# Sums of the down weights tied to the weight loads, one sum in place, and a new order of the pools in a hybrid encoder block

## Chip, cores and metric

The kernel runs on one core of a Trainium2 chip. The metric is the device time of one execution in microseconds. Engines: TensorE (PE, with its weight loads PEld), VectorE (DVE), ScalarE (ACT), GpSimd (POOL) and SyncE (SP), which only issues DMAs.

## What is computed

One layer over 2048 positions of width 1024, in float32:

```
h   = rms_norm(x) * norm_mix_g
z   = h @ w_in                       # two head groups share one projection
A   = u * (W_s LN(v) + b)            # gated blocks of 128 positions
B   = softmax(q k^T / 8 + c[t] - c[s]) v, s <= t,  c = cumsum(log sigmoid(f))
x   = x + concat(A, B) @ w_out
a   = conv3(rms_norm(x) * norm_ffn_g @ w_up) + b_conv     # 1024 -> 2 x 2816, causal, per channel
x   = x + (silu(g) * v) @ w_down     # a = g, v ; 2816 -> 1024
out = rms_norm(x) * norm_final_g
```

## The kernel before, in words

**Numbers as pairs.** Every float32 operand of a product is split in a rounded part and a remainder (`hi`, `lo`), and each product is made of three matmuls: hi.hi, hi.lo, lo.hi. The split is an ACT copy and a DVE subtraction (`both`, line 913) or, for weights of the first stages, a POOL cast `whi` and a DVE subtraction `wlo` (`load_unit`, line 118). `load_unit` takes a raw buffer (2 of them), loads it on SP and remembers that DMA as `raw_ins`; there are 4 buffers each for `whi` and `wlo`.

**Order of the work.** A schedule is made when the program is built: a list scheduler simulates the engines, starts each instruction as soon as its operands and a buffer of its tag are there, prefers the earlier one in the program (or one under `high_priority`), and fixes the order on each engine. On the chip each engine, SP's DMA issues included, keeps that order and waits where it must. `issue_after(ins)` puts the instructions traced inside behind `ins` in the order of the engine that `ins` runs on; it adds no semaphore.

**Stages.** First the input projection of two halves of 1024 positions (`a_half`). Attention runs as a stream of small steps (`b_stream`) put between the matmuls of the other stages. Then for half 0 the output projection (`c_half`, line 782): for two blocks of 512 positions it loads mixed values `thi`, `tlo` (`load_mix`), loads the output weights by `load_unit`, multiplies, adds the input rows, stores the result and makes normalised rows `ar` with a POOL instruction. Then the up projection of half 0 (`d_half`, line 853): 22 blocks `f` of 128 channels, each with a gate and a value unit of weights (`units(f)`, two `load_unit`) and two calls of `d_up` (one for each block of positions), with convolution and gate on DVE and ACT and a store of the gated values on POOL's queue.

**Sums of down weights.** The down projection uses Strassen's scheme in Winograd's form, seven products in place of eight, so it needs four sums of quarters of the down weights for each of 11 pairs of blocks. `d_sums(i)` (line 880) makes them on POOL: it loads two 512 KB tiles `tw` (2 buffers, so one pair at a time; lines 885, 886), subtracts four times (line 893) and stores each sum to DRAM on POOL's queue (line 894). In the program it stands between the two `d_up` calls of every second block (for the first and last pair of blocks, between the two blocks of positions).

**Half 1.** `c_late` (line 924) is the output projection of half 1; it reads mixed values 2 from the first pair of `thi`/`tlo` buffers and mixed values 3 from the second, and its weights through the same raw buffers. `late_half` (line 970) then makes an up projection in the seven-product form: `up_raw` (line 1052) loads raw weights `rawl` (3 buffers), `up_gate` splits the gate weights for products P1 and P2 (`xg`), `up_sums` (line 1064) makes four sums `sf` and splits them for the other five products (`xs`), and `up_mms` (line 1084) multiplies. Results are kept in `pc` tiles (3 buffers). The positions' own sums (`T1` to `T4`, `Y22`) are made once, at the beginning, on ACT and DVE.

The pools of half 1 are laid out in the order in which they are opened, in memory that the earlier stages held: before, the raw weights come first (kept open until the end of the program), then `xpool` (`xg`, then `xs`, then `sf`), `y2pool`, and the `pc` tiles last. A new tile waits for those tiles that lay in the same place. From the start of that memory, the earlier stages had 8 KB per partition of raw buffers, then 32 KB of the first `thi`/`tlo`, then 32 KB of the second, then the split weights.

**Down projection.** `down` (line 1147) runs for both halves the products P1, P2, P7, P6, P5, P4, P3, each over 11 units. `prep` (line 1172) loads a unit's weights or sums (`wr`), splits them (`wh`, `wl`), loads quarters of the gated values (`x11`, `x12`, `x21`, `x22`, 11 buffers each), adds them where the product asks for it, and splits them (`xh`, `xl`). `ready(u + 2)` keeps preparation two units ahead of the matmuls (line 1214).

Of the kernel before, what the change touches and what calls it, by code (L numbers as in the profile page):

```python
# [48 lines left out]
}  # L49
# [6 lines left out]
class Block:  # L56
# [823 lines left out]
    def d_sums(self, i):  # L880

        nc, dp = self.nc, self.dp
        w_down = self.a["w_down"][0].rearrange("(f p) n -> p f n", p=P)
        w1, w2 = self.til(dp, [P, D], F32, "tw"), self.til(dp, [P, D], F32, "tw")
        self.dma(w1, w_down[:, i, :])
        self.dma(w2, w_down[:, i + NF // 2, :])
        t1 = self.til(dp, [P, TB], F32, "tn")
        y11, y12 = w1[:, 0:TB], w1[:, TB:D]
        y21, y22 = w2[:, 0:TB], w2[:, TB:D]
        tt = nc.gpsimd.tensor_tensor  # L890

        for k, out, a, b in ((0, t1, y12, y11), (2, y12, y22, y12), (1, y22, y22, t1), (3, y21, y21, y22)):
            tt(out, a, b, op=ALU.subtract)
            nc.gpsimd.dma_start(self.tw_d[k][i], out)
# [75 lines left out]
    def late_half(self, accp, close_c):  # L970
        nc, tc = self.nc, self.tc
        self.c_late(accp)
        close_c()
        kw = dict(bufs=1, reuse_waits="tile")
        es = ExitStack()
        self.rawp = self.ctx.enter_context(tc.tile_pool(name="rawlate", **kw))
        xp = self.xp = es.enter_context(tc.tile_pool(name="xpool", **kw))
        yp = es.enter_context(tc.tile_pool(name="y2pool", **kw))
        self.up = es.enter_context(tc.tile_pool(name="upool", **kw))
        self.upp = es.enter_context(tc.tile_pool(name="ups", space=PSUM, **kw))  # L980
        self.w_up = self.a["w_up"][0].rearrange("(c p) n -> p c n", p=P)
        self.X, self.ps, self.p1, self.raw, self.cv = {}, {}, {}, {}, {}
        (y11, y21), (y12, y22) = self.yf
        y = lambda n: [yp.tile([P, 4, TB], F32R, name=f"{n}{i}") for i in "hl"]
        T2, T3, T1, T4, Y22 = y("t2"), y("t3"), y("t1"), y("t4"), y("y22")
        self.Y = dict(P1=self.Y11, P2=self.Y21, P3=Y22, P4=T4, P5=T1, P6=T2, P7=T3)
        for c in range(2):
            self.up_raw(0, c)
        self.up_raw(1, 0)
        self.up_gate(0)  # L990
        self.up_gate(1)
        self.prod(0, "P1", "A")
        self.prod(0, "P2", "C")
        self.up_sums(0)
        self.up_raw(2, 0)
        self.up_raw(1, 1)
        self.up_gate(2)

        def first(c):
            v = lambda t: t[:, :, c]  # L1000
            tt = nc.vector.tensor_tensor
            tt(v(y11), v(y12), v(y11), op=ALU.subtract)
            tt(v(y12), v(y22), v(y12), op=ALU.subtract)
            self.both([v(t) for t in Y22], v(y22))
            tt(v(y22), v(y22), v(y11), op=ALU.subtract)
            self.both([v(t) for t in T2], v(y22))

        first(slice(0, 384))
        for k in range(2):
            self.turned(1, 3, self.row, k, self.tqp, "tq")  # L1010
        first(slice(384, 512))
        self.prod(1, "P1", "A")
        self.prod(1, "P2", "C")
        self.both(T3, y12)
        self.both(T1, y11)

        nc.vector.tensor_tensor(y21, y21, y22, op=ALU.subtract)
        self.both(T4, y21)
        self.prod(2, "P1", "A")
        self.prod(2, "P2", "C")  # L1020
        for f in range(NF):
            self.up_mms(f)
            if 0 < f < NF - 1:
                self.up_conv(f - 1)
        es.close()
        self.tqs.close()
        self.down()
# [36 lines left out]
    def up_sums(self, f):  # L1064
        nc = self.nc
        g, v = self.raw.pop((f, 0)), self.raw.pop((f, 1))
        a, b = slice(0, 512), slice(512, 1024)
        S = {n: [self.til(self.xp, [P, TB], F32R, "xs" + n + i) for i in "hl"] for n in ("P6", "P7", "P5", "P4", "P3")}
        F = {n: self.til(self.xp, [P, TB], F32, "sf") for n in ("P5", "P6", "P3", "P7")}
        s = lambda n: F[n]  # L1070
        tt = nc.vector.tensor_tensor
        tt(s("P5"), v[:, a], v[:, b], op=ALU.add)
        tt(s("P6"), s("P5"), g[:, a], op=ALU.subtract)
        tt(s("P3"), g[:, b], s("P6"), op=ALU.subtract)
        self.both(S["P6"], s("P6"))
        tt(s("P7"), g[:, a], v[:, a], op=ALU.subtract)
        self.both(S["P7"], s("P7"))
        self.both(S["P5"], s("P5"))
        self.both(S["P4"], v[:, b])
        self.both(S["P3"], s("P3"))  # L1080
        for n in S:
            self.X[f, n] = S[n]
# [64 lines left out]
    def down(self):  # L1147
# [24 lines left out]
        def prep(u):  # L1172
            half, n, j = units[u]
            w = self.til(dp, [P, TB], F32, "wr")
            src = dict(P1=w_down[:, j, 0:TB], P2=w_down[:, j + NJ, 0:TB], P3=w_down[:, j + NJ, TB:D],
                       P5=self.tw_d[0][j], P6=self.tw_d[1][j], P7=self.tw_d[2][j], P4=self.tw_d[3][j])[n]
            self.w_ins = self.dma(w, src).ins
            wp = [self.til(dp, [P, TB], F32R, "wh"), self.til(dp, [P, TB], F32R, "wl")]
            self.both(wp, w)
            x = lambda name: block(half, j, name)  # L1180
            if n == "P1":
                v = x("x11")
            elif n == "P2":
                v = x("x12")
            elif n == "P7":
                v = self.til(dp, [P, TB], F32, "xs")
                tt(v, x("x11"), x("x21"), op=ALU.subtract)
            elif n == "P6":

                tt(x("x21"), x("x21"), x("x22"), op=ALU.add)  # L1190
                v = x("x11")
                tt(v, x("x21"), v, op=ALU.subtract)
            elif n == "P5":
                v = x("x21")
            elif n == "P4":
                v = x("x22")
            else:
                v = self.til(dp, [P, TB], F32, "xs")
                tt(v, x("x12"), x("x11"), op=ALU.subtract)
            xp = [self.til(dp, [P, TB], F32R, "xh"), self.til(dp, [P, TB], F32R, "xl")]  # L1200
            self.both(xp, v)
            parts[u] = wp, xp
# [55 lines left out]
        for half in range(2):  # L1258
            for n in self.PRODUCTS:
                which, blk, col, whole = PLAN[n]  # L1260
                fresh = n in ("P1", "P2", "P7")
                if fresh:
                    banks[which] = [self.til(pp, [P, TB], F32, "D") for _ in range(4)]
                bank = banks[which]
                tail = {"P2": 2, "P6": 2, "P3": 4 if half else 2}.get(n, 0)
                cs = slice(col * TB, (col + 1) * TB)
                for j in range(NJ - tail):
                    ready(u + 2)
                    for t in range(4):
                        mms(bank, u, t, fresh, j == NJ - 1)  # L1270
                    u += 1
                    if (n, j) == ("P1", 4):
                        for t in range(4):
                            row(half, t)
                    if (n, j) == ("P2", 7):
                        for t in range(4):
                            row(half, 4 + t)
                for t in range(4):
                    if tail:
                        ready(u + tail + max(0, t - 1))  # L1280
                    for m in range(tail):
                        mms(bank, u + m, t, fresh, m == tail - 1)
                    x = row(half, 4 * blk + t)
                    tt(x[:, cs], bank[t], x[:, cs], op=ALU.add)
                    if whole:
                        square(half, 4 * blk + t, col)
                        if n in ("P4", "P3"):
                            end_row(half, 4 * blk + t)
                u += tail
# [55 lines left out]
```

## Time and profile before

| | |
|---|---|
| runs | 2522.92, 2529.30, 2529.84 us; median 2529.3 |
| profiled execution | 2528.71 us, of which the span from first to last instruction is 2527.0 |
| mean granted TensorE clock | 0.992 of 2.4 GHz |
| busy, share of the span | PE 97%, PEld 79%, DVE 69%, ACT 54%, POOL 14% |
| DMA | 396 MB, mean 157 GB/s |

PE's busy share is an average over stages; what matters is in which stages it has pauses and what ended them. The granted clock of a stretch is 1.00 when TensorE ran at 2.4 GHz all through it, and 0.5 at 1.2 GHz. Each wait is put down to what released it last.

### The profile page before, as it was taken

To read this page: it belongs to the slowest core of one execution; us is meant where nothing else is said; L and a number is where in the kernel's file an instruction comes from. 1 tells how busy PE (TensorE), PEld (TensorE's weight loads), DVE (VectorE), ACT (ScalarE), POOL (GpSimd) and SP (SyncE) were. 2 spreads that over 40 slices of the span, in tenths; PEclk is the share of its full clock that TensorE was granted. 3 is DMA by queue.
4 is the path that set the end of the run, shared out by engine and by line. 5 is a ranking of instruction groups with operands and counts; after the bars stand their busy time and mean duration, and the time that the engine had idled before them with its cause. 6 is when DMAs were issued, how large, how long until landed. Compare 5 with 4: busy or idle time off the path is not lost.

```text
span 2527.0 us, 33250 instructions
## 1 busy us (share of the span) xinstructions
PE 2448.3 (97%) x11082; PEld 1998.6 (79%) x11082; DVE 1750.6 (69%) x3119; ACT 1360.0 (54%) x2628; POOL 360.1 (14%) x402
## 2 busy tenths in 40 slices
PE   8999989999999999999999999989999999999997
PEld 6887877878777788888888888868888887888886
DVE  5237676565556877777777775488888877858766
ACT  4327777554344555667676672254554455444443
POOL 3204122000356511100010011100000000001000
PEclk9999999999999999999999999999999999999999
DMA  6863534666978744444444445412222227538633
GB/s 184 261 163 100 165 110 123 182 174 190 303 263 274 237 130 130 142 140 136 136 140 147 138 125 193 157 53 81 92 84 79 88 93 275 167 97 308 189 110 113
DMA packets 348567, 396.10 MB, mean 157 GB/s; under 512 B 53964, under 2 KB 223124, under 8 KB 348380
## 3 DMA queue, kind: packets, MB, share of 16 engines
q1 hardware_dynamic: 338188, 359.37, 46.9%
q0 software_dynamic: 10208, 34.61, 3.5%
q8 instruction: 88, 1.44, 0.2%
q14 instruction: 83, 0.68, 0.1%
HBM read 300.30 MB, written 93.72 MB: 156 GB/s over the span
## 4 chain that ended last, share of the span: by engine, by line
PE 79%; DMA 7%; DVE 5%; ACT 4%; POOL 2%; issue 2%; SPq 0%; POOLq 0%; DVEq 0%; ACTq 0%
PE D L1214 17%; PE mm L174 11%; PE mm L176 11%; PE mm L178 11%; PE A L1043 3%; PE A L1042 3%; PE A L1044 3%; PE o L722 2%; PE o L721 2%; DMA tw<-in_w_down_dram 2%; PE B L1043 2%; PE B L1044 2%; PE B L1042 2%; PE s L673 2%; PE s L672 1%
## 5 line engine op out<-in xcount | busy, mean ns | idle before, releaser
L174 PE MATMUL mm<-thi,whi 128*128 128x512 f32 x960 | 378.5, 394 | 1.3 <-DVE vn L384 1.3
L178 PE MATMUL mm<-thi,wlo 128*128 128x512 f32 x960 | 377.6, 393 | 0.9 <-DVE wlo L128 0.9
L176 PE MATMUL mm<-tlo,whi 128*128 128x512 f32 x960 | 377.3, 393 | 0.0
L174 PE MATMUL mm<-whi,thi 128*128 128x512 f32 x640 | 254.2, 400 | 7.1 <-DMA thi<-mixh 3.1
L176 PE MATMUL mm<-wlo,thi 128*128 128x512 f32 x640 | 254.7, 398 | 2.7 <-DVE wlo L128 2.6
L178 PE MATMUL mm<-whi,tlo 128*128 128x512 f32 x640 | 253.5, 396 | 0.0
L1214 PE MATMUL D<-wh,xh 128*128 128x512 f32 x616 | 236.2, 389 | 3.0 <-ACT xh L915 3.0
L1214 PE MATMUL D<-wl,xh 128*128 128x512 f32 x616 | 236.7, 389 | 0.0
L1214 PE MATMUL D<-wh,xl 128*128 128x512 f32 x616 | 235.9, 389 | 0.0
L681 ACT ACTIVATE s<-s,part 128x512 f32<-128x512 f32 (+3 forms) x257 | 150.5, 586 | 141.6 <-DVE part L676 81.9
L174 PEld LDWEIGHTS mm<-thi,whi 128*128 128x128 f32 x960 | 181.0, 189 | 40.2 <-DVE vn L384 2.0
L178 PEld LDWEIGHTS mm<-thi,wlo 128*128 128x128 f32 x960 | 180.9, 188 | 39.0 <-DVE wlo L128 1.4
L176 PEld LDWEIGHTS mm<-tlo,whi 128*128 128x128 f32 x960 | 181.1, 189 | 37.8
L116 POOL TENSOR_SCALAR whi<-raw 128x1024 fp32r<-128x1024 f32 x108 | 121.5, 1126 | 621.6 <-PE mm L178 200.5
L128 DVE TENSOR_TENSOR wlo<-raw,whi 128x1024 fp32r<-128x1024 f32 x108 | 138.6, 1284 | 59.3 <-POOL whi L116 59.1
L745 DVE TENSOR_TENSOR pl<-e,ph 128x512 fp32r<-128x512 f32 (+2 forms) x212 | 139.5, 666 | 55.6 <-ACT ph L744 31.2
L739 ACT ACTIVATE e<-s 128x512 f32<-128x512 f32 (+2 forms) x227 | 115.4, 528 | 107.4 <-DVE s L737 56.6
L174 PEld LDWEIGHTS mm<-whi,thi 128*128 128x128 f32 x640 | 121.3, 190 | 33.5 <-POOL whi L116 4.0
L176 PEld LDWEIGHTS mm<-wlo,thi 128*128 128x128 f32 x640 | 121.6, 190 | 28.8 <-DVE wlo L128 5.8
L178 PEld LDWEIGHTS mm<-whi,tlo 128*128 128x128 f32 x640 | 121.2, 190 | 23.9
L1214 PEld LDWEIGHTS D<-wh,xh 128*128 128x128 f32 x616 | 115.5, 188 | 27.5 <-ACT xh L915 3.4
L1214 PEld LDWEIGHTS D<-wl,xh 128*128 128x128 f32 x616 | 115.5, 188 | 24.2 <-DVE wl L916 0.4
(1092 smaller groups left out, 5566.7 us busy)
## 6 DMA issues: line engine op xcount, KB each, us to landing
m<-kx SPq DMA_DIRECT2D x133, 256.0 KB
raw<-in_w_up_dram SPq DMA_DIRECT2D x44, 512.0 KB
rawl<-in_w_up_dram SPq DMA_DIRECT2D x44, 512.0 KB
x<-act SPq DMA_DIRECT2D x88, 256.0 KB
wr<-tw SPq DMA_DIRECT2D x88, 256.0 KB
m<-kx SPq DMA_DIRECT2D x160, 136.0 KB
raw<-in_w_in_dram SPq DMA_DIRECT2D x40, 512.0 KB
v<-vd SPq DMA_DIRECT2D x66, 256.0 KB
```

Source lines behind the costliest of these rows:

```text
L116: self.cast_ins = self.nc.gpsimd.tensor_scalar(out, in_, 1.0, 0.0, ALU.mult, ALU.add).ins
L128: nc.vector.tensor_tensor(lo, raw, f32(hi), op=ALU.subtract)
L174: mm(ps, lhsT=ah[k], rhs=bh[k], start=k == 0, stop=False)
L176: mm(ps, lhsT=ah[k], rhs=bl[k], start=False, stop=False)
L178: mm(ps, lhsT=al[k], rhs=bh[k], start=False, stop=k == n - 1)
L681: nc.scalar.activation(ps[:, :n], ps[:, :n], AF.Exp, scale=-1.0, bias=dst, accum_out=ls[:, tt, sb:sb + 1])
L739: nc.scalar.activation(e[:, c], ps[:, c], AF.Exp, scale=-1.0)
L745: nc.vector.tensor_tensor(pl[:, c], e[:, c], f32(ph[:, c]), op=ALU.subtract)
L1042: mm(ps, lhsT=xh[:, ks], rhs=yh[:, k, :], start=fresh and k == 0, stop=False, **kw)
L1043: mm(ps, lhsT=xh[:, ks], rhs=yl[:, k, :], start=False, stop=False, **kw)
L1044: mm(ps, lhsT=xl[:, ks], rhs=yh[:, k, :], start=False, stop=k == 3, **kw)
L1214: nc.tensor.matmul(bank[t], lhsT=x[i][:, ts], rhs=w[k], start=fresh and j == 0 and i + k == 0, stop=last and i == 1, **kw)
```

## The change

The two `tw` loads of `d_sums` are issued behind the last raw weight load traced before them. In `late_half`, the pool of the `pc` tiles is opened first, the pool of the raw weights second, and the latter now closes with the others; the four `sf` tiles are allocated before the `xs` tiles; `pc` has 4 buffers. In `prep`, the difference `x12 - x11` is written into `x12` during product P5, and P3 uses it from there. In product P3 of half 1, preparation runs four units ahead.

```
-    ... "pc": 3, "A": 3, "B": 1, "C": 3,
+    ... "pc": 4, "A": 3, "B": 1, "C": 3,
@@ d_sums
-        self.dma(w1, w_down[:, i, :])
-        self.dma(w2, w_down[:, i + NF // 2, :])
+
+        with self.tc.issue_after(self.raw_ins):
+            self.dma(w1, w_down[:, i, :])
+            self.dma(w2, w_down[:, i + NF // 2, :])
@@ late_half
-        self.rawp = self.ctx.enter_context(tc.tile_pool(name="rawlate", **kw))
+
+        self.up = es.enter_context(tc.tile_pool(name="upool", **kw))
+        self.rawp = es.enter_context(tc.tile_pool(name="rawlate", **kw))
         xp = self.xp = es.enter_context(tc.tile_pool(name="xpool", **kw))
         yp = es.enter_context(tc.tile_pool(name="y2pool", **kw))
-        self.up = es.enter_context(tc.tile_pool(name="upool", **kw))
@@ up_sums
+        F = {n: self.til(self.xp, [P, TB], F32, "sf") for n in ("P5", "P6", "P3", "P7")}
         S = {n: [self.til(self.xp, [P, TB], F32R, "xs" + n + i) for i in "hl"] for n in ("P6", "P7", "P5", "P4", "P3")}
-        F = {n: self.til(self.xp, [P, TB], F32, "sf") for n in ("P5", "P6", "P3", "P7")}
@@ prep
             elif n == "P5":
                 v = x("x21")
+
+                tt(x("x12"), x("x12"), x("x11"), op=ALU.subtract)
             elif n == "P4":
                 v = x("x22")
             else:
-                v = self.til(dp, [P, TB], F32, "xs")
-                tt(v, x("x12"), x("x11"), op=ALU.subtract)
+                v = x("x12")
@@ down
-                    ready(u + 2)
+                    ready(u + (4 if (half, n) == (1, "P3") else 2))
```

## Rows read from the trace of the kernel before

**Rows 1.** The page's chain that ended last, by line.

```profile
PE D L1214 17%; PE mm L174 11%; PE mm L176 11%; PE mm L178 11%; PE A L1043 3%; PE A L1042 3%; PE A L1044 3%; PE o L722 2%; PE o L721 2%; DMA tw<-in_w_down_dram 2%; PE B L1043 2%; PE B L1044 2%; PE B L1042 2%; PE s L673 2%; PE s L672 1%
```

**Rows 2.** Stages: length, busy PE PEld DVE ACT POOL (instructions), clock, DMA share, GB/s.

```profile
668.00:796.00 128.00, 118.96 (x525) 94.73 (x524) 74.20 (x132) 54.18 (x125) 73.64 (x72) 0.96 0.83 269
796.00:889.00 93.00, 85.46 (x370) 67.89 (x369) 76.40 (x112) 49.21 (x100) 50.01 (x52) 0.94 0.76 242
889.00:1510.00 621.00, 621.00 (x2811) 511.84 (x2810) 468.22 (x971) 424.50 (x936) 59.15 (x72) 1.00 0.45 137
1645.00:1695.00 50.00, 38.72 (x167) 29.71 (x165) 43.75 (x53) 23.64 (x32) 1.30 (x2) 0.93 0.15 47
2095.00:2513.00 418.00, 417.69 (x1843) 345.52 (x1841) 304.04 (x509) 197.56 (x367) 11.94 (x16) 1.00 0.57 185
870.00:882.00 12.00, 9.32 (x29) 7.10 (x28) 11.45 (x17) 4.81 (x10) 4.91 (x7) 0.72 0.69 221
```

**Rows 3.** Waits of PE, 640 to 905 us: total us, times, longest.

```profile
PE o L722 <- DVE pl L745: 4.7, 4, 2.7
PE mm L174 <- DMA thi<-mixh: 3.1, 1, 3.1
...
PE s L672 <- DMA t<-cc: 2.6, 1, 2.6
```

**Rows 4.** Waits of SP's DMA issues, 640 to 905 us.

```profile
SPq L74 <- DMA tw<-tw: 71.4, 16, 7.2
```

**Rows 5.** Chain of waits around one pause: start, us, what.

```profile
857.98 6.96 DMA tw<-in_w_down_dram
...
869.06 1.03 POOL whi L116
...
870.11 2.91 DVE wlo L128
...
874.35 0.79 PE o L722
```

**Rows 6.** Sums on line 893: ns min/median/max, first and last start; POOL busy in a stage.

```profile
L893 POOL TENSOR_TENSOR tw<-tw x11: 1286/1302/2019, 689.2 to 887.4; 128x512 f32<-128x512 f32 x11
...
796.00:889.00 93.00, 28.88 (x20) 0.94 0.76 242
```

**Rows 7.** SP's issues of raw up weights: start, us.

```profile
796.32 5.11 SPq L74 DMA_DIRECT2D raw<-in_w_up_dram  x2
...
856.55 0.38 SPq L74 DMA_DIRECT2D raw<-in_w_up_dram  x1
```

**Rows 8.** POOL in order of time: two casts of the up projection.

```profile
1024.02 1.05 POOL L116 TENSOR_SCALAR whi<-raw 128x1024 fp32r<-128x1024 f32 x1 [6.54 <-issue]
...
1053.30 1.04 POOL L116 TENSOR_SCALAR whi<-raw 128x1024 fp32r<-128x1024 f32 x1 [4.97 <-PE mm L176]
```

**Rows 9.** DVE in order of time: one convolution step, beside a sum and alone.

```profile
847.91 2.30 DVE L841 SCALAR_TENSOR_TENSOR t<-a,colA,t 128x512 f32<-128x512 f32 x1
...
856.45 0.74 DVE L841 SCALAR_TENSOR_TENSOR t<-a,colA,t 128x512 f32<-128x512 f32 x1
```

**Rows 10.** Down projection: the sum for P3 by line, and a stretch of P5.

```profile
L1199 DVE TENSOR_TENSOR xs<-x,x 128x512 f32<-128x512 f32 x22 | 14.8, 682 | 0.0
...
2205.00:2230.00 25.00, 25.00 (x112) 20.71 (x111) 13.95 (x22) 10.43 (x19) 0.00 (x0) 1.00 0.36 96
```

**Rows 11.** In order of time, end of the output projection: DVE, SP, DVE, PE, PE.

```profile
1601.89 0.69 DVE L947 TENSOR_TENSOR acc<-mm,acc 128x512 f32<-128x512 f32 x1 [2.58 <-PE mm L178]
...
1630.94 3.19 SPq L74 DMA_DIRECT2D rawl<-in_w_up_dram  x3
...
1649.63 0.68 DVE L1072 TENSOR_TENSOR sf<-rawl 128x512 f32<-128x512 f32 x1
...
1673.16 0.49 PE L1042 MATMUL B<-t3h,xsP7h 128*128 128x512 f32 x1 [2.64 <-ACT t3h L915]
...
1678.09 0.79 PE L1043 MATMUL B<-t3l,xsP7h 128*128 128x512 f32 x1 [3.67 <-DVE t3l L916]
```

**Rows 12.** PE in order of time: the down projection's first matmuls.

```profile
2093.28 1.20 PE L1214 MATMUL D<-wh,xh 128*128 128x512 f32 x4 [3.00 <-ACT xh L915]
```

2 rows, old and new, of the table BUFS are left out of this document.

## The prediction

> **What bounds the kernel now.** I read the chain of waits first: TensorE (PE) holds most of it, but the loads `tw<-in_w_down_dram`, which feed sums that only the down projection reads, a millisecond later, are 2% of the span by themselves [rows 1]. So those sums sit on the path. I then cut the span into stages [rows 2]. Look at PE busy against the length of the stage, and at the granted clock. From 889 to 1510 us PE is busy for all of 621 us at clock 1.00, and from 2095 to 2513 for 417.69 of 418. The losses sit at a few places; the three that the change touches most are:
>
> - 668 to 796 us: 128 - 118.96 = 9.0 us idle, and a clock of 0.96, that is 0.04 x 128 = 5.1 us: 14.2 us.
> - 796 to 889 us: 93 - 85.46 = 7.5 us idle, and 0.06 x 93 = 5.6 us: 13.1 us.
> - 1645 to 1695 us: 50 - 38.72 = 11.3 us idle, and 0.07 x 50 = 3.5 us: 14.8 us.
>
> The clock term is TensorE at 1.2 instead of 2.4 GHz for some microseconds after a pause; 870 to 882 us shows one, 2.68 us without work and then a mean of 0.72, which costs 0.28 x 12 = 3.4 us more [rows 2, 5].
>
> Third, who ended PE's waits near the first two stretches [rows 3]: a DVE result, and loads (`thi`, `t`) that merely came late. Why late, the queue of SP tells [rows 4]: it stood 71.4 us in 16 waits, up to 7.2 us each, for stores `tw<-tw`. A load of the next sum needs the buffer that the last sum is still storing; SP issues in order, so everything behind that load stood too. The chain of one pause [rows 5] shows the second way: the weight load lands at 864.9, POOL does its sums, the cast `whi` stands behind them in POOL's order, the DVE's `wlo` waits for the cast, `pl` stands behind `wlo`, and PE waits for `pl`.
>
> All 11 sums run from 668 to 889 us [rows 6]: the loads are free to go as soon as a buffer is, so the scheduler puts them together at the end of the first output projection and the start of the up projection.
>
> **Part 1, the sums.** Removed: nothing. 22 loads, 44 POOL subtractions and 44 stores are moved. Each pair of loads now goes behind the second weight load of its own pair of blocks on SP. Those stood at about 796.3 us (first of the two issues in that row: block 1) and 856.6 us (block 3) [rows 7], then once per two blocks. So 2 of the 11 sums stay ahead of 889 us and 9 go into 889 to 1510 us, 621 / 9 = 69 us apart.
>
> What it gives: from 668 to 796 us no sum is left. Of the 14.2 us I keep 2 as an estimate for waits that the ordinary work (output rows, mixed values, attention) makes there, and count 12.2 as gained. From 796 to 889 us five sums ran (20 subtractions [rows 6]), 13.1 / 5 = 2.6 us each; two stay, 5.2 us, so 7.9 us are gained. Together 20.1 us. Ends: 0, if something else that is late takes the place of each wait, to all 27.3.
>
> What it costs later: 9 sums in a stage where PE has no idle time to give. On SP a load then never waits for a store of its own kind (69 us between sums; today 221 / 11 = 20 us do for one), so the 71.4 us of rows 4 go. On POOL, 59.15 us of 621 are used [rows 2]; 9 sums add 9 x 4 x 1.3 = 47 us. The queue behind a sum holds the next cast and the stores of gated values; the second weight load goes out when the second cast of the block before has freed its buffer, and the next cast follows 29 us later (1024.02 and 1053.30 us [rows 8]), so the sum falls between casts, unlike at 869 us [rows 5]. On DVE: a sum makes DVE instructions that overlap it longer, 2.30 us where the same instruction takes 0.74 alone [rows 9]. The Trainium skill says why (SBUF — State Buffer, "Who interferes with whom"): a DVE instruction with two SBUF inputs contends with a GpSimd instruction that reads SBUF, and the later one blocks fully. By that rule DVE would lose up to 4 x 1.3 = 5.2 us per sum; these rows agree with it. Whether PE sees it is another matter: DVE is busy 468.22 of 621 us there, and the sum that ran from 840 to 852 us stretched DVE (the first of rows 9 is in it) and left no pause on PE: the next one is that of rows 5. I therefore take 0 per sum, from that nearest case; the other end is 2.6 us each, 23.6 us, the mean price of today's crowd. Below nothing is excluded: no PE idle time is there to be gained.
>
> **Part 2, the sum in place.** 22 subtractions of 0.68 us [rows 10] move from product P3 to P5, into a tile that is there anyway; no instruction more or less. In P5 (2205 to 2230 us) DVE is busy 13.95 of 25 us [rows 10]; 11 x 0.68 = 7.5 us over some 30 us of one product fits, and PE has no idle time in the whole stage [rows 2]. The two units more of preparation at the very end of P3 ease a DVE that already keeps up. 0; ends 0 to a loss of 15 us (all 22 uncovered), which the 11 us of slack per 25 excludes.
>
> **Part 3, placement.** The first raw weights of the second up projection now lie where the mixed values of block 2 were, which PE has read when the eighth of that stage's 16 products is added, at 1601.89 us [rows 11], instead of where the raw output weights are; today their loads start at 1630.94 us [rows 11]. The working tiles `sf` move from memory that the last output products still read to memory free since then. Today all of this is done in the crowd: DVE runs almost without a break from 1649.63 to the result that PE waits for at 1678.09 [rows 11]. Seven of its instructions there need only early data after the change: the four `sf` sums of block 0 (the first of them in rows 11) and three `xg` remainders. At a pitch of 0.60 us they are 4.2 us, and DVE was mostly idle before. The two pauses that end there are 2.64 and 3.67 us [rows 11]; they shrink by those 4.2 us, and I take half of the 3.5 us of clock, 1.7. Gain 5.9 us; next late is the same DVE chain, now the column sums. The `xs` tiles move the other way, onto memory read until 1649 us; only one of their casts (0.6 us, on ACT) ran earlier than that. Ends: 0 (nothing starts earlier) to 9.
>
> The raw pool is also released earlier, so the down tiles slide down. At the start of the down projection PE pauses 3.00 us for a cast on ACT [rows 12], which stood in ACT's own order, not behind a buffer. I take 0; ends -2 to +3, since new neighbours end later or sooner by about one product. The fourth `pc` buffer can only take waits away: 0.
>
> **Sum.** 20.1 + 5.9 = 26.0 us. The profiled execution took 2528.7 us (span 2527.0 and 1.7 around it), so it would take 2502.7. The median of the three runs is 0.6 above it: 2503.3, given as 2503.
>
> **Rivals.**
> - The price moves along with the sums: each of the 9 later sums costs its 2.6 us of today, 23.6 us. Then 2503.3 + 23.6 = 2526.9, no change. For it: DVE is 75% busy there and PE has no slack. Against: SP's waits and the chain of rows 5 come from crowding, and a lone sum at 840 us left no pause. Chance 0.10.
> - The later sums hold up DVE and slow the kernel: in 889 to 1510 us every sum puts a cast and `wlo` behind it as at 869 us, PE waits 2.68 us for `pl` and then runs 3.4 us slower, 6.1 us each, 55 us. 2503.3 + 55 = 2558, slower. It decides the sign from 26 / 9 = 2.9 us per sum. For it: rows 5 show it once, and DVE's stretched steps show the hold [rows 9]. The Trainium skill's rule above (SBUF — State Buffer, "Who interferes with whom") speaks for it too. Against: it needs a cast due while a sum holds POOL, and in the even stage casts lie 29 us apart where a sum would come [rows 8]. Chance 0.06.
> - The change doesn't do what it says: the second weight loads go early too, the sums stay together, only part 3 gives its 5.9 us: 2523.4, no change. Against: rows 7, since those loads wait for the casts before them. Chance 0.04.
>
> **How the numbers follow.** The forecast, sums spread at little cost, has 0.80, all of it faster; a measurement of this kernel can tell about 0.3%, 7.6 us. With a share of the first rival that ends half way: faster 0.81, within 0.3% 0.13, slower 0.06. Range: down to 2491, where all 27.3 us, 9 at the boundary and 2 at the down projection go (38.3); up to 2520, where part 1 gives 9 us less and part 3 next to nothing, or half the later sums cost as today. Left out are the slower rival and most of the other two.
>
> **What would show it.** Right: subtractions on POOL spread from about 790 to 1510 us; SP's wait for `tw<-tw` gone; PE idle in 668 to 889 us under 6 us, with no stretch at half clock or one; PE still fully busy to 1510 us; raw up weights issued near 1600 us; the two pauses in block 0's product P7 (2.64 and 3.67 us today) about 4 us shorter in sum. Wrong: pauses on PE for `pl` right after sums in the later stage (first or second rival); the sums together again; or the waits for `thi`, `t` and `m` still there without sums beside them, which would mean that attention, not the crowd, made them late.

## The result and the profile after

| | before | after |
|---|---|---|
| median of five runs of each | 2529.84 us (2522.92 to 2534.22) | 2506.89 us (2505.06 to 2512.34) |
| profiled execution, span | 2528.71, 2527.0 us | 2508.73, 2507.0 us |
| DVE busy, share of the span | 69% | 71% |

The ratio is 0.9916, interval 0.9896 to 0.9936: 22.9 us faster, against 26.0 predicted. The forecast 2503 is 4 us off, inside its range of 2491 to 2520.

To see where the time went, I pick matmuls that both kernels have at the ends of stages, and compare their starts. First PE in order of time before: the last attention wait ahead of the sums, and the first transpose after the last output product (its third anchor, 2093.28, is in [rows 12]).

```profile
652.32 0.50 PE L672 MATMUL s<-m,t 96*128 96x512 f32 x1 [1.04 <-ACT s L681]
...
1651.06 0.63 PE L149 MATMUL dn<-ident,ar 128*128 128x128 f32 x4 [1.20 <-DVE cv L921]
```

The same view after, with the pauses of block 0's P7 (1650.61, 1655.09) and every pause between the first two anchors:

```profile
653.33 0.50 PE L672 MATMUL s<-m,t 96*128 96x512 f32 x1 [2.03 <-ACT s L681]
...
717.15 0.50 PE L174 MATMUL mm<-whi,thi 128*128 128x512 f32 x1 [0.69 <-DMA thi<-mixh]
719.19 0.50 PE L178 MATMUL mm<-whi,tlo 128*128 128x512 f32 x1 [0.96 <-DMA tlo<-mixl]
...
798.64 0.50 PE L722 MATMUL o<-pl,v 128*128 128x512 f32 x1 [1.36 <-DVE pl L745]
...
1627.72 0.63 PE L149 MATMUL dn<-ident,ar 128*128 128x128 f32 x4 [1.20 <-DVE cv L923]
...
1650.61 0.79 PE L1045 MATMUL B<-t3h,xsP7h 128*128 128x512 f32 x1 [3.43 <-ACT t3h L917]
...
1655.09 0.80 PE L1046 MATMUL B<-t3l,xsP7h 128*128 128x512 f32 x1 [2.74 <-DVE t3l L918]
...
2070.46 0.80 PE L1218 MATMUL D<-wh,xh 128*128 128x512 f32 x1 [3.00 <-ACT xh L917]
```

Between the anchors:

- to the first anchor: 653.33 - 652.32, 1.0 us later;
- first to second, where the sums were and now are: 974.4 instead of 998.7 us, 24.4 us shorter;
- second to third, half 1's up projection with the new placement: 442.7 instead of 442.2, 0.5 us longer;
- third to the end: 436.5 instead of 433.7, 2.8 us longer.

Together 20.0 us, the difference of the spans. The gain is all in the stretch of the sums. The windows after, to be laid beside [rows 2] (columns as there; the fourth is the output boundary, the fifth the start of the down projection):

```profile
668.00:796.00 128.00, 126.12 (x584) 102.51 (x583) 76.20 (x145) 62.15 (x139) 35.94 (x34) 1.00 0.68 215
796.00:889.00 93.00, 91.60 (x423) 74.89 (x424) 78.61 (x138) 56.13 (x117) 21.90 (x26) 1.00 0.54 172
889.00:1510.00 621.00, 620.74 (x2809) 510.95 (x2808) 498.58 (x965) 420.92 (x929) 123.24 (x139) 1.00 0.50 161
1620.00:1670.00 50.00, 38.83 (x166) 29.73 (x166) 42.69 (x53) 24.44 (x33) 1.47 (x2) 0.90 0.17 53
2062.00:2082.00 20.00, 17.00 (x64) 13.48 (x63) 18.49 (x23) 12.37 (x19) 1.06 (x2) 0.83 0.85 274
```

PE's idle time in 668 to 889 us fell from 16.6 to 3.3 us, and the clock there is 1.00 where it was 0.95. From 889 to 1510 us POOL does twice as much as before (59.15, now 123.24), DVE 30.4 us more, and PE stands 0.26 us. The last line is where 2.8 us were lost: after the same pause of 3.00 us, TensorE ran for some microseconds at 1.2 GHz (clock 0.83 over 20 us); in the profiled execution of before it did not (1.00 from 2085 to 2105 us).

The sums themselves, by line, and SP's issues of the `tw` loads before 889 us:

```profile
L895 POOL TENSOR_TENSOR tw<-tw x11: 1294/1305/1312, 796.1 to 1456.7; 128x512 f32<-128x512 f32 x11
```

```profile
778.14 2.28 SPq L74 DMA_DIRECT2D tw<-in_w_down_dram  x2
...
834.94 0.86 SPq L74 DMA_DIRECT2D tw<-in_w_down_dram  x2
...
880.01 1.01 SPq L74 DMA_DIRECT2D tw<-in_w_down_dram  x2
```

The last subtractions of the sums start from 796 to 1457 us, where [rows 6] had 689 to 887. Three pairs of loads, not two, go out ahead of 889 us, and two and a half sums run there (the third begins at 884.88): the raw loads behind which they stand come sooner when SP does not stand. SP's wait for `tw<-tw` (71.4 us in [rows 4]) is gone.

### The profile page after: what moved, and what is told of

The parts are those of the page before. It is cut to its first block, busy times and chain, and to the rows that moved or that the text cites. A ratio compares the mean times of both kernels' runs of the same rounds, so it can differ in the third digit from the quotient of the medians.

```text
span 2507.0 us, 33220 instructions
## 1 busy us (share of the span) xinstructions
PE 2442.7 (97%) x11082; PEld 1995.9 (80%) x11082; DVE 1771.5 (71%) x3119; ACT 1360.1 (54%) x2628; POOL 357.9 (14%) x402
## 4 chain that ended last, share of the span: by engine, by line
PE 84%; DMA 4%; DVE 4%; ACT 3%; issue 2%; POOL 1%; SPq 1%; POOLq 0%; DVEq 0%; ACTq 0%
PE D L1218 17%; PE mm L174 12%; PE mm L176 12%; PE mm L178 12%; PE A L1046 3%; PE A L1045 3%; PE A L1047 3%; PE o L722 2%; PE o L721 2%; PE s L673 2%; PE s L672 2%; PE s L734 2%; PE s L733 2%; PE B L1046 2%; PE B L1047 2%
## 5 line engine op out<-in xcount | busy, mean ns | idle before, releaser
L917 ACT ACTIVATE xh<-x 128x512 fp32r<-128x512 f32 x132 | 82.3, 628 | 120.4 <-PE D L1218 108.4
L918 DVE TENSOR_TENSOR xl<-x,xh 128x512 fp32r<-128x512 f32 x132 | 90.3, 688 | 75.8 <-ACT xh L917 72.1
```

What stands on the lines that cost most here:

```text
L918: self.nc.vector.tensor_tensor(parts[1], x, f32(parts[0]), op=ALU.subtract)
```

## Experiments

Every ratio is against the kernel before on the same chip, with its interval. Where two experiments are compared by medians, they ran on one chip.

### 1. Is it the sums, and the sums alone?

`e1_sums_only`: the kernel before with only the two loads tied.

```
-        self.dma(w1, w_down[:, i, :])
-        self.dma(w2, w_down[:, i + NF // 2, :])
+        with self.tc.issue_after(self.raw_ins):
+            self.dma(w1, w_down[:, i, :])
+            self.dma(w2, w_down[:, i + NF // 2, :])
```

> The kernel before with the first part of the change alone (the two tw loads behind the last raw weight load). My theory after the two traces: this part gives all of the gain; 2505 to 2510 us, PE idle in 668 to 889 us under 5 us. Rival, as the prediction had it: the placement brings 5.9 us of the gain, so this kernel would stand 4 to 7 us above the changed one, at 2511 to 2514 us.

Measured: 2507.24 us, ratio 0.9901 (0.9886 to 0.9916).

`e2_without_sums_part`: the changed kernel with these loads free again, so parts 2 and 3 alone.

```
-        with self.tc.issue_after(self.raw_ins):
-            self.dma(w1, w_down[:, i, :])
-            self.dma(w2, w_down[:, i + NF // 2, :])
+        self.dma(w1, w_down[:, i, :])
+        self.dma(w2, w_down[:, i + NF // 2, :])
```

> The changed kernel with the tw loads free to go early again, all other parts kept. My theory: the other parts give nothing, 2527 to 2532 us, and the sums stand together from 668 to 889 us with PE idle about 16 us there. Rival: placement and the sum in place give some us, 2520 to 2525 us.

Measured: 2531.12 us, ratio 1.0000 (0.9991 to 1.0009). The stretch of the sums, first `e1_sums_only`:

```profile
668.00:889.00 221.00, 220.02 (x1025) 180.97 (x1024) 151.79 (x284) 118.71 (x257) 58.59 (x59) 1.00 0.64 203
```

and `e2_without_sums_part`:

```profile
668.00:889.00 221.00, 204.93 (x915) 163.81 (x914) 155.82 (x248) 103.13 (x225) 121.98 (x123) 0.98 0.81 263
```

PE's idle time, 1.0 against 16.1 us, follows the loads. The two loads are the whole gain; the sum in place and the placement give nothing together.

### 2. What in the crowd cost the time?

Three edits of the kernel before, all with the sums still together ahead of 889 us. Its stretch, to lay theirs beside:

```profile
668.00:889.00 221.00, 204.42 (x893) 162.62 (x892) 150.60 (x244) 103.39 (x225) 123.65 (x124) 0.95 0.80 258
```

`e4_loads_on_pool_queue` takes SP's standing away and leaves the rest, but for the issues, which now stand in POOL's order (8.8 us there until a store is done):

```
-        self.dma(w1, w_down[:, i, :])
-        self.dma(w2, w_down[:, i + NF // 2, :])
+        nc.gpsimd.dma_start(w1, w_down[:, i, :])
+        nc.gpsimd.dma_start(w2, w_down[:, i + NF // 2, :])
```

> The kernel before, with the two loads of each sum issued on POOL's queue, so that SP's issues never stand behind a buffer of the sums; the eleven sums stay together before 889 us. If it was the standing of SP's queue (71.4 us) that cost most of the 23 us, PE's waits for thi and t in 640 to 905 us go, idle time in 668 to 889 us falls from 16.6 us to under 8, and the time is 2510 to 2520 us. If the crowd on POOL and DVE cost it (casts behind sums, wlo and pl behind the casts), the waits for pl stay, idle time stays over 12 us and the time is 2526 to 2533 us. I lean to the second, 0.6.

Measured: 2523.41 us, ratio 0.9975 (0.9965 to 0.9986), between the two expectations. Its stretch, and PE's waits from 640 to 905 us:

```profile
668.00:889.00 221.00, 206.12 (x923) 164.47 (x923) 152.91 (x251) 104.35 (x227) 123.05 (x140) 0.98 0.80 263
```

```profile
PE s L672 <- ACT s L681: 4.9, 2, 2.7
PE mm L174 <- DVE acc L808: 2.3, 1, 2.3
PE o L722 <- DVE pl L745: 1.9, 1, 1.9
...
PE mm L174 <- DMA thi<-mixh: 0.7, 1, 0.7
```

The late loads (`thi` 3.1 us, `t` 2.6 us in [rows 3]) shrink or go, but PE is idle 14.9 us where it was 16.6: waits for ACT and DVE came in their place. Most of the gain is in the clock, 0.98 against 0.95.

`e9_before_no_subtractions` leaves out the sums' arithmetic on POOL and keeps loads and stores, for which SP stands:

```
-            tt(out, a, b, op=ALU.subtract)
-            nc.gpsimd.dma_start(self.tw_d[k][i], out)
+            nc.gpsimd.dma_start(self.tw_d[k][i], a)
```

> The kernel before without the 44 subtractions on POOL: a loaded quarter is stored in place of each sum, with the same loads and stores (so the sums of the down weights are left out). What remains of the crowd is SP's standing and the DMA traffic. If POOL's arithmetic and its hold on DVE cost the time, 668 to 889 us lose under 8 us of idle time and the time is 2508 to 2518 us. If SP's standing or the traffic cost it, the waits for thi and t stay and the time is 2523 to 2531 us. My theory: the first, most of the 23 us, 0.65.

Measured: 2517.50 us, ratio 0.9944 (0.9928 to 0.9961).

```profile
668.00:889.00 221.00, 215.71 (x994) 174.97 (x993) 135.12 (x269) 111.95 (x241) 61.56 (x83) 1.00 0.82 279
```

Idle time falls to 5.3 us and the clock is 1.00, with as much DMA traffic as before (0.82) and SP still standing, though 47.1 us for stores where it was 71.4: this edit takes some of SP's standing away too.

`e12_crowd_of_dmas_alone` makes both edits; POOL's order then stands 29.8 us for stores.

> The kernel before without the 44 subtractions (a loaded quarter is stored in place of each sum, so the sums of the down weights are left out) and with the loads of the pairs issued on POOL's queue: what remains of the crowd before 889 us is the DMA traffic. If POOL's arithmetic (12.4 us without it) and SP's standing (6.5 us with the loads elsewhere) are two separate costs, they add up: 2529.9 - 18.9 = 2511 us. If either hides the other, 2515 to 2518 us; if together they make up the whole, with the traffic free, 2503 to 2507 us. I expect the first, 2508 to 2514 us.

Measured: 2512.35 us (four runs, 2510 to 2521), ratio 0.9929 (0.9904 to 0.9955). What is left shows in its stretch:

```profile
668.00:889.00 221.00, 210.52 (x967) 172.18 (x966) 134.48 (x268) 110.47 (x237) 72.19 (x99) 0.98 0.80 268
```

So by the medians POOL's arithmetic was the larger part of the crowd's price (12.4 us) and SP's standing the smaller (6.5 us); both together gave 19.3. That is near their sum, 18.9, but the intervals of the last two ratios overlap, and PE's idle time in this stretch (10.5 us) is above that of `e9_before_no_subtractions`. The first two anchors speak against a sum. In `e9_before_no_subtractions`:

```profile
659.24 0.80 PE L672 MATMUL s<-m,t 96*128 96x512 f32 x1 [3.19 <-ACT s L681]
...
1638.00 0.63 PE L149 MATMUL dn<-ident,ar 128*128 128x128 f32 x4 [1.20 <-DVE cv L920]
```

That is 978.8 us, 20.0 shorter than before. `e4_loads_on_pool_queue` takes 991.8 us (from 654.45 to 1646.21), 7.0 shorter, and `e12_crowd_of_dmas_alone` 982.5 (from 654.39 to 1636.92), 16.2 shorter. In the profiled execution of `e9_before_no_subtractions` the first anchor comes 6.9 us later than before, ahead of the first load of a sum (674.8 us), which hides part of its gain in the whole time. So leaving out the arithmetic gave more than moving the loads, by the ratios too, whose intervals lie apart. How the two costs combine stays open.

### 3. What does a spread sum cost, and from where?

`e11_after_no_subtractions`, `e10_sums_half_again` and `e3_sums_twice` put 0, 6 and 8 subtractions into each sum of the changed kernel instead of 4, with the same DMAs. `e3_sums_twice`:

```
+            tt(self.til(dp, [P, TB], F32, "twice"), a, b, op=ALU.subtract)
             tt(out, a, b, op=ALU.subtract)
```

`e10_sums_half_again` does that for `k in (0, 1)` only; `e11_after_no_subtractions` has the edit of `e9_before_no_subtractions`.

> The changed kernel without the 44 subtractions on POOL, with the same loads and stores (the sums of the down weights are left out): the point with no POOL arithmetic beside the up projection. If a lone sum is absorbed by the lead that attention has, as the lack of pauses in the changed kernel says, the time is the changed kernel's within 3 us, 2503 to 2509 us, while DVE's busy time from 889 to 1510 us falls by about 30 us, to some 468. If part of the price is there after all, under 2502 us.

> The changed kernel with two of the four subtractions of each sum made a second time into a scratch tile (results and DMAs the same): half of the work that the doubling added. If the price grows evenly with POOL's time, half of the doubling's 22.5 us: 2518 us. If it is a lead that is used up, nearly nothing until it is gone: 2507 to 2512 us, with few waits for pl from 889 to 1510 us. I expect the second, 0.65.

> The changed kernel with each of the 44 subtractions done twice on POOL, the first time into a scratch tile that nobody reads; results and DMAs are the same. If a lone sum costs PE nothing in the even stage (my forecast), the time stays at 2506 to 2509 us, and DVE only gets busier between 889 and 1510 us, by up to 9 x 5.2 = 47 us. If PE sees the hold on DVE (the first rival), 9 sums at up to 2.6 us each, 2515 to 2530 us.

The medians are not all of one chip; the ratios are what compares.

| subtractions per sum | median, us | ratio | PE idle 668 to 889 | PE idle 889 to 1510 |
|---|---|---|---|---|
| 0 | 2503.06 | 0.9892 (0.9877 to 0.9907) | 0.7 | 0.0 |
| 4 (changed kernel) | 2506.89 | 0.9916 (0.9896 to 0.9936) | 3.3 | 0.26 |
| 6 | 2514.47 | 0.9942 (0.9927 to 0.9957) | 4.1 | 4.6 |
| 8 | 2529.35 | 0.9989 (0.9980 to 0.9998) | 7.0 | 8.4 |

The windows from 889 to 1510 us with 0, 6 and 8:

```profile
889.00:1510.00 621.00, 621.00 (x2815) 512.09 (x2814) 463.06 (x966) 423.78 (x927) 72.80 (x101) 1.00 0.50 160
```

```profile
889.00:1510.00 621.00, 616.36 (x2778) 506.11 (x2777) 505.26 (x956) 416.39 (x926) 147.34 (x157) 1.00 0.51 161
```

```profile
889.00:1510.00 621.00, 612.58 (x2747) 500.23 (x2746) 512.54 (x946) 414.27 (x920) 176.98 (x177) 1.00 0.52 163
```

The price bends. Without subtractions DVE's busy time falls to 463.06 us, and time and clock hardly change: the first four subtractions are nearly free (the intervals of 0 and 4 overlap). The next four cost 22.1 us (2529.35 against the 2507.24 of `e1_sums_only` on the same chip). PE is idle 6.0 us more than in `e1_sums_only` ahead of 889 us and 8.4 us more behind it. My theory for the doubling, free, was wrong, and for the half step I expected too little (2507 to 2512). An even price between four and eight is not excluded: half way between the ratios of `e1_sums_only` and `e3_sums_twice` lies 0.9945, inside the interval of the half step. The bend that shows is at four. `e3_sums_twice` shows what happens beyond it. First POOL, then DVE, then PE in order of time around 1317 us:

```profile
1315.93 1.32 POOL L896 TENSOR_TENSOR tw<-tw,tw 128x512 f32<-128x512 f32 x1
1317.22 1.73 POOL L895 TENSOR_TENSOR twice<-tw,tn 128x512 f32<-128x512 f32 x1
```

```profile
1316.01 1.79 DVE L745 TENSOR_TENSOR pl+_2765_12062<-e,ph+_2764_12061 128x512 fp32r<-128x512 f32 x1
1317.73 1.78 DVE L841 SCALAR_TENSOR_TENSOR t<-a,colA,t 128x512 f32<-128x512 f32 x1
1319.43 1.93 DVE L745 TENSOR_TENSOR pl+_2769_12077<-e,ph+_2768_12076 128x512 fp32r<-128x512 f32 x1
1321.29 2.26 DVE L849 SCALAR_TENSOR_TENSOR t<-a,t 128x512 f32<-128x512 f32 x1
1323.47 1.75 DVE L745 TENSOR_TENSOR pl<-e+_2771_12086,ph 128x512 fp32r<-128x512 f32 x1
1325.14 0.68 DVE L745 TENSOR_TENSOR pl<-e,ph 128x512 fp32r<-128x512 f32 x1
```

```profile
1325.28 0.67 PE L722 MATMUL o<-pl,v 128*128 128x512 f32 x1 [1.97 <-DVE pl L745]
```

The first five DVE steps take 1.75 us or more each where such a step takes 0.68 or 0.74 alone, and POOL's subtraction goes up to 1.73 from 1.3: the two engines take turns. After some 13 us of it PE waits 1.97 us for the `pl` made at 1323.47, and TensorE runs at 1.2 GHz for about 3.4 us (clock 0.57 from 1325 to 1329 us). With four subtractions the hold is the same but ends after two or three steps (in the changed kernel 1.78, 2.14 and 1.98 us around 1307 us), and PE does not wait. I read this as a lead of attention's own work that covers the shorter hold; no run measured the lead itself.

Is it the hold, or merely a busier POOL with casts and stores behind it? Two kernels replace the doubling by filling a scratch tile with zeros ten times per sum, which keeps POOL as busy and reads nothing.

> The changed kernel in which POOL, beside each sum, fills a scratch tile with zeros ten times (0.53 us each, 5.3 us in all) where the doubling made four more subtractions (5.2 us); results and DMAs the same. POOL is as busy as in the doubled kernel, but the added work reads nothing. If the 22.5 us of the doubling came from DVE instructions held by POOL's reads, DVE's busy time from 889 to 1510 us stays near 500 us, PE has few waits for pl, and the time is 2507 to 2511 us. If they came from POOL's own order (casts and stores behind a longer sum), it is 2522 to 2530 us like the doubled kernel. My theory: the first, 0.75.

`e13_memsets_beside_sums` came to 2510.78 us, ratio 0.9919 (0.9893 to 0.9945), but does not tell the theories apart: the fills depend on nothing, the scheduler took all 110 to before 889 us, and POOL did no more after it than in the changed kernel. `e14_memsets_in_the_sums` ties them to their place:

```
+            last = tt(out, a, b, op=ALU.subtract)
+            z = self.til(dp, [P, TB], F32, "twice")
+            with self.tc.issue_after(last.ins):
+                for _ in range(3 if k in (0, 1) else 2):
+                    nc.gpsimd.memset(z, 0.0)
```

> As the kernel with memsets, but the fills are put behind their subtraction in POOL's order, so that they can't run ahead in the first stretch: ten fills of 0.53 us, 5.3 us more of POOL per sum, at the place where the doubling had 5.2 us of subtractions. If the doubling's 22.5 us came from DVE instructions held by POOL's reads, DVE's busy time from 889 to 1510 us stays near 500 us with POOL's near 175, there are few waits for pl, and the time is 2507 to 2513 us. If they came from POOL's order, 2522 to 2530 us. My theory: the first, 0.75.

Measured: 2512.23 us, ratio 0.9918 (0.9894 to 0.9943). Its window, then POOL and DVE around 1308 us:

```profile
889.00:1510.00 621.00, 620.58 (x2810) 511.07 (x2809) 494.92 (x966) 421.21 (x929) 164.70 (x228) 1.00 0.52 161
```

```profile
1307.62 3.47 POOL L899 MEMSET twice<- 128x512 f32 x6
```

```profile
1304.86 2.37 DVE L841 SCALAR_TENSOR_TENSOR t<-a,colA,t 128x512 f32<-128x512 f32 x1
...
1307.93 0.69 DVE L849 SCALAR_TENSOR_TENSOR t<-a,t 128x512 f32<-128x512 f32 x1
1308.54 0.68 DVE L745 TENSOR_TENSOR pl<-e+_2771_12116,ph 128x512 fp32r<-128x512 f32 x1
```

The ratio is that of the changed kernel (0.9916). POOL is busy 164.70 us, most of the way to the doubled kernel's 176.98, and PE stands 0.42 us. DVE is held to 2.37 us by a subtraction and takes its normal 0.68 beside the fills. So the doubling's price came from reads that hold DVE, not from POOL being busy. (Six of the ten fills of the sum shown run behind its last store, at 1307.06, so the stores are held up less than in the doubled kernel; that part of POOL's order is not tested.) The Trainium skill has that rule (SBUF — State Buffer, "Who interferes with whom"): a DVE instruction with two SBUF inputs contends with a GpSimd instruction that reads SBUF, not with one that only writes it. The trace agrees with both halves, 2.37 and 0.68 us.

### 4. Why did the placement give nothing?

In the changed kernel SP does issue the first raw up weights early, but what should follow from it did not move. SP, ACT and DVE in order of time, after:

```profile
1579.03 1.01 SPq L74 DMA_DIRECT2D rawl<-in_w_up_dram  x2
```

```profile
1623.13 0.61 ACT L917 ACTIVATE xgP1h<-rawl 128x512 fp32r<-128x512 f32 x1
```

```profile
1626.29 0.68 DVE L1075 TENSOR_TENSOR sf<-rawl 128x512 f32<-128x512 f32 x1
```

The weights have their first cast some 44 us after their issue. My theory: the scheduler holds everything of a pool until all memory that the pool covers is free, and `xpool` still covers the second `thi`/`tlo`, read until the last output product. `e7_own_pool` gives `xg` and `sf` a pool that lies in the first pair alone:

```
+        self.xg = es.enter_context(tc.tile_pool(name="xgpool", **kw))
-            x = ... self.til(self.xp, [P, TB], F32R, "xg" + name + i) ...
+            x = ... self.til(self.xg, [P, TB], F32R, "xg" + name + i) ...
-        F = {n: self.til(self.xp, [P, TB], F32, "sf") ...
+        F = {n: self.til(self.xg, [P, TB], F32, "sf") ...
```

> The changed kernel with the xg and sf tiles in a pool of their own, which covers exactly the memory of the first thi and tlo, so that nothing in this pool lies on memory that is read until the end of the output projection. My theory: the schedule holds back whatever is in a pool until all of the memory that the pool covers is free, and that is why the seven DVE instructions of part 3 did not move; now they stand in the idle time before, and the pauses of 3.43 and 2.74 us in product P7 shrink by 4 us in sum, 2501 to 2504 us. Rival: the order comes from the landing of the loads or from ACT's and DVE's own order; then nothing moves, 2506 to 2508 us.

Measured: 2505.79 us, ratio 0.9891 (0.9875 to 0.9908). ACT, DVE and PE in order of time:

```profile
1585.60 0.63 ACT L917 ACTIVATE xgP1h<-rawl 128x512 fp32r<-128x512 f32 x1 [3.50 <-issue]
...
1635.82 1.15 ACT L962 ACTIVATE ar<-acc,rstd 128x1024 f32<-128x1024 f32 x1 [4.74 <-POOL rstd L143]
```

```profile
1588.19 0.69 DVE L1076 TENSOR_TENSOR sf<-rawl 128x512 f32<-128x512 f32 x1 [0.64 <-DMA rawl<-in_w_up_dram]
```

```profile
1637.02 0.66 PE L149 MATMUL tq<-ident,ar 128*128 128x128 f32 x4 [0.25 <-ACT ar L962]
...
1649.90 0.49 PE L1046 MATMUL B<-t3h,xsP7h 128*128 128x512 f32 x1 [2.71 <-ACT t3h L917]
1654.38 0.80 PE L1047 MATMUL B<-t3l,xsP7h 128*128 128x512 f32 x1 [3.23 <-DVE t3l L918]
```

The casts and sums now run some 38 us earlier, which bears out the pool. But the two pauses still add up to 5.94 us (6.17 in the changed kernel). One chain that ends there comes down from the last output row, through its scale on POOL, its normalisation on ACT (1635.82) and the transposes (1637.02) to the column sums. The profile's own chain of waits goes another way, over a raw weight load of the next block (3.90 us from 1632.47) and the `sf` sum behind it (1636.40). Which of them sets the pauses was not tried. From the second anchor to the third it takes 2.6 us less than the changed kernel. By medians it is 1.45 us ahead of `e1_sums_only`: the fastest kernel here that leaves nothing out, but not by more than can be measured.

## Why the prediction was right, step by step

**What bounds the kernel: right.** The sums sat on the path, and tying their loads took away all that the change gained (`e1_sums_only`, `e2_without_sums_part`).

**Part 1: right, the term too small.** 20.1 us were predicted and 24.4 came between the anchors. I left 2 us of the first stretch and 5.2 of the second; 1.9 and 1.4 us of idle time remained, and no half clock. The 5.2 were mis-sized: I priced a sum that stays at the 2.6 us it cost in the crowd, and alone it costs PE little. Of the 3.3 us of idle time in both, 1.65 stand at 717 and 719 us, ahead of the first sum (787.0), and 1.36 at 798.64, beside it; in `e1_sums_only`, with the loads tied in the same way, all of it is 1.0 us. The reason, too, was incomplete. Of the two mechanisms, SP's standing and POOL's arithmetic, I leaned on SP first; by experiment 2 the arithmetic is the larger.

**Price of the later sums: right, with less room than I thought.** I took 0 per sum, and PE stood 0.26 us in 621. The hold on DVE was there, 30.4 us for eight and a half sums (34 of the 44 subtractions start behind 889 us), 3.6 each, against the 5.2 that I had as an upper bound. The first two rivals fell because PE does not see one hold of that length. Experiment 3 shows how near they were: with eight subtractions the gain is gone (0.9989), by the mechanism that the second rival named, `pl` behind a held DVE, though not behind a cast.

**Part 2: right.** In `e2_without_sums_part` it costs nothing measurable. PE is busy 412.61 of the 413 us from 2080 to 2493 us, while the 22 subtractions run in product P5:

```profile
L1199 DVE TENSOR_TENSOR x<-x,x x22: 675/682/686, 2153.5 to 2395.9; 128x512 f32<-128x512 f32 x22
```

**Part 3: wrong, 5.9 us predicted, none came.** The step that failed is "Seven of its instructions there need only early data after the change". Early data were there at 1579 us, but the instructions also needed tiles of a pool that covers memory still being read. And the next step, "they shrink by those 4.2 us", would have failed too: in `e7_own_pool` the seven do run early (1586 to 1593 us), and the pauses are only 0.2 us shorter than in the changed kernel.

**Down projection's start: 0 predicted; the pause is the same 3.00 us.** The 2.8 us in the profiled execution are clock after that pause. `e4_loads_on_pool_queue`, which has no part 3, shows the same clock loss there (0.83 from 2080 to 2100 us), so I do not put it down to the placement.

The sum came out near because part 1's missing 4.3 us made good most of part 3's 5.9. That is luck: the two errors have nothing to do with each other.

## What to carry to other kernels

Work that is only needed much later should be tied to something with the pace of the stage that has to absorb it, not merely be free to go when a buffer is. Before you call a hold on another engine free, double it: a price that is near zero at one size and 22 us at twice the size shows how little room was left. And when a tile is placed in memory that comes free early, ask what else the same pool covers.

## What the runs showed that I had not expected

- POOL and DVE hold each other by turns: in the doubled kernel POOL's subtraction rose to 1.73 us from 1.3 while DVE's steps rose to 1.75 from 0.68.
- The price of POOL's reads to PE is bent: 0.0, 0.26, 4.6 and 8.4 us of idle time from 889 to 1510 us for 0, 4, 6 and 8 subtractions per sum, so next to nothing up to four and some 4 us for each two beyond.
- 106.7 us of POOL work in the 221 us from 668 to 889 us cost little when 54.7 of it only wrote (`e13_memsets_beside_sums`, 0.9919). In the crowd of before POOL had 123.7 us without such fills, but SP's standing and the loads came on top there.
